# Low parts of weights on one engine, head factors inside the gates' product, four PSUM banks for the second half's gates, and a written order at the first modulation

## The chip, the cores and the metric

The kernel runs on one core of a Trainium2 chip. The metric is device time in microseconds for one execution, from launch to the last byte of the output in memory; of several executions the median is taken. The engines are named as in the profile: PE (TensorE) multiplies matrices and PEld loads its weights, DVE (VectorE) and ACT (ScalarE) do arithmetic on tiles, POOL (GpSimd) is the third engine that can do it, SP (SyncE) issues most DMAs. Each engine works through its own list of instructions strictly in order.

## The reference: what is computed

A decoder of two layers on 1024 tokens of width 1024, in float32. Cut to what matters here:

```python
cond = jax.nn.silu(c)
for l in range(DEPTH):                                   # l = 0: mixer A, l = 1: mixer B
    ada = cond @ ada_w[l] + ada_b[l]                     # six vectors of 1024
    sh1, sc1, g1, sh2, sc2, g2 = jnp.split(ada, 6, axis=-1)
    h = modulate(rmsnorm(x, norm_g[l, 0]), sh1, sc1)     # h * (1 + sc1) + sh1
    y = mlstm_mixer(h, ...) if l < N_A else mla_mixer(h, ..., k_nope, k_rope, v)
    x = x + g1 * rmsnorm(y, norm_g[l, 1])
    h = modulate(rmsnorm(x, norm_g[l, 2]), sh2, sc2)
    x = x + g2 * rmsnorm(jnp.square(jax.nn.relu(h @ w1)) @ w2, norm_g[l, 3])

# end of mlstm_mixer: q, k, v, ig, fg, og are columns of h @ w_in
hh = rmsnorm(hh.transpose(0, 2, 1, 3), head_g).reshape(B_, S, A_V_W)
return (hh * jax.nn.sigmoid(og)) @ w_out
```

Mixer A is a chunked mLSTM with 8 heads, mixer B a causal attention with 8 heads in which 128 queries at a time meet all earlier keys. `head_g` is one factor for each of the 1024 columns of `hh`.

## The kernel before

**Products in three passes.** Every operand of a large product is held as two numbers: a high part, which is the value cast to the type that PE multiplies, and a low part, which is the value minus the high part. One product is then three matmuls (`mm3`, lines 236 to 238): low times high, high times low, high times high. For a weight chunk of 128 by 1024 numbers (`raw`, 512 KB, brought by SP at L216) `wsplit` makes the two parts: ACT casts the high part `wh` (L193), and the low part `wl` is a subtraction (L195). Which engine subtracts is set by `low[0]`: DVE, POOL, or, while it is `None`, DVE and POOL by turns. It is set to DVE for the first weights, in the first MLP of the first half, and in the norms and projections of layer 1, to POOL in the attention of layer 1, and is `None` elsewhere. For activations `split_mod` does the same with a shift added: ACT writes the high part (L478), DVE the low part (L479).

**Halves and streams.** The 1024 tokens are worked on as two halves of 512 (`hfs[0]`, `hfs[1]`). Projections of a half run as "steps" of 128 output columns: 24 matmuls of 128x512 into one PSUM bank. Layer 0's mixer of the first half comes first, then that of the second half beside the first half's output projection; from the first MLP on, `two_streams` weaves a dense stream (an MLP of one half) with a second stream (the norms, projections and attention of the other half), and a third one of small background work is spread between (the adaLN products of later layers: chunks of `raw` multiplied by the conditioning vector on DVE, L363 and L365, summed by PE at L345 and DVE at L347).

**What sets the order.** The program is written as generators that are advanced by turns, and a planner puts each engine's instructions in order by a timeline that it keeps; `tc.high_priority` and `tc.issue_after(x)` (this instruction stands after x in the order) steer it. So a change of the engine of one operation moves others too. On the chip nothing is moved any more.

**PSUM.** There are three kinds of tiles, two of each: `ps` and `pc` of one bank, `pm` of two banks. `wout` (L890) with `wide` takes `ps` and the first bank of `pm` by turns, so that four steps are open at once.

**The four places of the change.**

- `wsplit` as above, with `follow[0]`: while it is set, the latest subtraction on DVE is what background work is paced by.
- `og0` (L671): the eight steps of the output gate of layer 0. Each step's product goes to a `ps` bank; ACT reads it (L676, exp), then does L677 (ln) and L678 (exp) in SBUF, which gives the sigmoid; DVE multiplies the tile by the head factor, a column of `cols` (L679). `split_o` (L786) later multiplies the mixer's output by the gate in blocks of two heads (L792, 128x1024), ACT casts the high part (L793), and DVE or POOL by turns subtracts (L794).
- `latent_weights` (L1153): six chunks are scaled by a row factor on POOL.
- `modulate0` (L1651): the first modulation. For each k, DVE multiplies x by the norm and the scale (L1655), and `split_mod` follows. The shift is the column `adac(0, SH1)`, which a DVE addition at L341 delivers (`ada`).

## Time and profile before

Three runs: median 2408.23 us (2406.89 to 2409.44). One execution was profiled.

| | before |
|---|---|
| median of 3 runs | 2408.23 us |
| the profiled execution's own time | 2411.54 us |
| its span (first to last instruction) | 2409.7 us |
| PE busy | 2367.1 us (98%) |
| DVE busy | 1481.7 us (61%) |
| ACT busy | 1051.8 us (44%) |
| POOL busy | 414.1 us (17%) |
| DMA, mean over the span | 155 GB/s |

The profiled execution took 1.84 us more than its span and 3.3 us more than the median; sums made from the trace are compared with 2411.54, and then carried over to the median. "Busy" of PE counts from the start of a matmul to its modelled end, and matmuls overlap, so 98% says that PE seldom stands, not that it runs at its peak. Line numbers are those of the kernel before; in the changed kernel the same lines stand two lines earlier up to the gates (L479 is L477 there), one earlier in the attention (L1128 is L1127), and L1655 is L1657.

### The profile page before, as it was taken

Reading aid. Unit: us, or ns where it says so; the run is one execution under the profiler, and the core shown is the slowest. Engines: PE = TensorE matmul, PEld = TensorE weight load, DVE = VectorE, ACT = ScalarE, POOL = GpSimd, SP = SyncE. Lnnn points to the kernel's source line nnn. Section 1 sums busy time; section 2 is a strip of 40 time slices with the busy share of each in tenths; the row PEclk is TensorE's granted clock in tenths of the full one; section 3 lists DMA queues with packets and bytes.
Section 4 is the critical chain, followed back from the end, with each engine's and each line's share of the span. In section 5 each row is a group of like instructions: output and inputs, shape, how many; then the busy total and the mean of one; then the engine's idle time right before and its main releaser. Section 6 shows DMA issues by size and latency. Waiting matters only on the chain.

```text
span 2409.7 us, 30573 instructions
## 1 busy us (share of the span) xinstructions
PE 2367.1 (98%) x11621; PEld 1947.3 (81%) x11621; DVE 1481.7 (61%) x2271; ACT 1051.8 (44%) x1712; POOL 414.1 (17%) x259
## 2 busy tenths in 40 slices
PE   7999999999999999999999999999999999999998
PEld 5888888788888887888888878888888888888887
DVE  6667766868665667866754967654555385253335
ACT  4355334555333454434443554434444443443333
POOL 2121111200000000234321100332221102121121
PEclk9999999999999999999999999999999999999999
DMA  8452654444654745455543444763424454354431
GB/s 305 144 149 81 188 179 132 144 144 149 184 175 140 249 131 189 153 164 179 181 131 114 144 163 161 238 241 133 158 97 137 116 162 123 109 188 133 144 104 62
DMA packets 377107, 374.49 MB, mean 155 GB/s; under 512 B 24355, under 2 KB 282464, under 8 KB 376960
## 3 DMA queue, kind: packets, MB, share of 16 engines
q1 hardware_dynamic: 376672, 372.44, 48.5%
q8 instruction: 92, 1.51, 0.3%
q14 instruction: 55, 0.45, 0.1%
q0 software_dynamic: 288, 0.10, 0.0%
HBM read 313.24 MB, written 59.24 MB: 155 GB/s over the span
## 4 chain that ended last, share of the span: by engine, by line
PE 89%; DVE 5%; DMA 3%; ACT 2%; issue 1%; SPq 0%; POOL 0%; DVEq 0%; ACTq 0%
PE ps L236 16%; PE ps L237 16%; PE ps L238 16%; PE pm L236 10%; PE pm L237 10%; PE pm L238 10%; DMA raw<-in_mlp_w_dram 1%; PE pc L1449 1%; PE pc L236 1%; PE pm L819 1%; PE pc L237 1%; PE pc L238 1%; PE pm L1335 1%; PE pm L1329 1%; PE pm L1331 1%
## 5 line engine op out<-in xcount | busy, mean ns | idle before, releaser
L193 ACT CAST wh<-raw 128x1024 fp32r<-128x1024 f32 (+2 forms) x366 | 375.8, 1031 | 724.0 <-PE ps L236 341.0
L195 POOL TENSOR_TENSOR wl<-raw,wh 128x1024 fp32r<-128x1024 f32 (+2 forms) x158 | 375.6, 2381 | 1558.6 <-ACT wh L193 1407.1
L236 PE MATMUL ps<-k,wl 128*128 128x512 f32 x1528 | 612.6, 401 | 6.1 <-ACT k L676 4.4
L237 PE MATMUL ps<-k,wh 128*128 128x512 f32 x1528 | 602.5, 394 | 0.0
L238 PE MATMUL ps<-k,wh 128*128 128x512 f32 x1528 | 602.4, 394 | 0.0
L195 DVE TENSOR_TENSOR wl<-raw,wh 128x1024 fp32r<-128x1024 f32 (+1 forms) x208 | 270.6, 1304 | 275.3 <-ACT wh L193 267.9
L236 PEld LDWEIGHTS ps<-k,wl 128*128 128x128 f32 x1528 | 288.0, 188 | 74.1 <-issue 7.2
L238 PEld LDWEIGHTS ps<-k,wh 128*128 128x128 f32 x1528 | 288.0, 188 | 67.6 <-issue 0.5
L237 PEld LDWEIGHTS ps<-k,wh 128*128 128x128 f32 x1528 | 288.3, 189 | 63.7 <-issue 1.7
L203 DVE TENSOR_TENSOR k<-k,pm 128x512 f32<-128x512 f32 (+1 forms) x254 | 210.5, 858 | 129.4 <-PE pm L238 128.8
L476 DVE TENSOR_TENSOR hd<-tmp,hd 128x512 fp32r<-128x512 f32 x128 | 120.7, 943 | 208.4 <-ACT hd L475 208.0
L236 PE MATMUL pm<-hd,wl 128*128 128x512 f32 x512 | 202.0, 394 | 0.5 <-ACT hd L475 0.5
L237 PE MATMUL pm<-hd,wh 128*128 128x512 f32 x512 | 199.4, 390 | 0.7 <-DVE hd L476 0.7
L238 PE MATMUL pm<-hd,wh 128*128 128x512 f32 x512 | 199.8, 391 | 0.0
L236 PE MATMUL pm<-wh,hd 128*128 128x512 f32 x488 | 193.0, 395 | 4.4 <-ACT raw L1341 4.2
L237 PE MATMUL pm<-wl,hd 128*128 128x512 f32 x488 | 190.9, 391 | 0.0
L238 PE MATMUL pm<-wh,hd 128*128 128x512 f32 x488 | 190.4, 390 | 0.0
L365 DVE SCALAR_TENSOR_TENSOR tma<-raw,cond,tma 128x512 f32<-128x512 f32 x168 | 129.1, 769 | 19.9 <-DMA raw<-in_kv_ada_w_dram 10.1
L1341 ACT ACTIVATE raw<-pm,sm 128x128 f32<-128x128 f32 (+3 forms) x64 | 47.5, 742 | 156.1 <-DVE sm L1340 126.8
L237 PEld LDWEIGHTS pm<-hd,wh 128*128 128x128 f32 x512 | 96.2, 188 | 21.7 <-DVE hd L476 1.0
L236 PEld LDWEIGHTS pm<-hd,wl 128*128 128x128 f32 x512 | 96.1, 188 | 21.2 <-ACT hd L475 0.9
L238 PEld LDWEIGHTS pm<-hd,wh 128*128 128x128 f32 x512 | 96.1, 188 | 21.1
(351 smaller groups left out, 3580.0 us busy)
## 6 DMA issues: line engine op xcount, KB each, us to landing
raw<-in_mlp_w_dram SPq DMA_DIRECT2D x256, 512.0 KB, 4.2
raw<-in_ada_w_dram SPq DMA_DIRECT2D x80, 512.0 KB, 4.3
raw<-in_a_w_in_dram SPq DMA_DIRECT2D x48, 512.0 KB, 4.6
xs<-k SPq DMA_DIRECT2D x40, 256.0 KB, 4.6
raw<-in_kv_ada_w_dram SPq DMA_DIRECT2D x16, 512.0 KB, 3.9
raw<-in_a_w_out_dram SPq DMA_DIRECT2D x16, 512.0 KB, 4.6
kd<-k SPq DMA_DIRECT2D x32, 256.0 KB, 3.7
vd<-k SPq DMA_DIRECT2D x32, 256.0 KB, 4.4
```

The lines of the kernel that those rows point to most:

```text
L193: nc.scalar.copy(hi[:, :n], r[:, :n])
L195: i = e.tensor_sub(lo[:, :n], r[:, :n], hi[:, :n].bitcast(F32))
L203: return f(*a, **k)
L236: nc.tensor.matmul(o, ll, rh, start=start, stop=False)
L237: nc.tensor.matmul(o, lh, rl, start=False, stop=False)
L238: pe_last[0] = nc.tensor.matmul(o, lh, rh, start=False, stop=stop)
L365: nc.vector.scalar_tensor_tensor(acc, r[:, kk], cond[:, k : k + 1], acc, ALU.mult, ALU.add)
L476: nc.vector.tensor_sub(lo, u, hi.bitcast(F32))
L819: nc.tensor.matmul(nv[:, r, i], hf.PT[p_][:, r, cs], v[:, 2 * p_ + r], start=g == 0, stop=True,)
L1329: nc.tensor.matmul(o[:, :w], ql, kh, start=True, stop=False)
L1331: nc.tensor.matmul(o[:, :w], qT, kk[1][:, ks], start=False, stop=False)
L1341: nc.scalar.activation(pr[:, :n], f, AF.Exp, bias=m, scale=SCALE, accum_out=l)
```

## The change

- Every `wl` is subtracted by DVE (`low` and `wcnt` are gone), and so are the second and fourth block of L794. The scaling of the six latent weights moves from POOL to DVE. POOL then has no arithmetic left but the setting of constants: its list has 96 rows where it had 264, DVE's has 2433 where it had 2273.
- The multiplication by the head factors (L679, 16 instructions of 128x512) goes. `split_o` does it in the same instruction as the gate: two `scalar_tensor_tensor` of 128x512 take the place of one product of 128x1024.
- `one_pm` names the first bank of a `pm` tile. In the second half, the odd steps of `og0` go there, the even ones to `ps`; in the first half all go to `ps` as before.
- `modulate0` writes down DVE's order: within a block of four k, the second product is put behind the addition that delivers the shift, the third behind the first low part, the fourth behind the second low part.

The diff, whole:

```diff
--- before.py
+++ after.py
@@ -153,6 +153,9 @@
     def pm():
         return pp.tile([P, 2, 512], F32, tag="pm", bufs=2, name=f"pm_{next(uid)}")
 
+    def one_pm():
+        return pm()[:, 0]
+
     def const(shape, dt, name):
         return sb.tile(shape, dt, tag=name, bufs=1, name=name)
 
@@ -183,17 +186,12 @@
 
         return tc.issue_after(pace[0]) if pace[0] else nullcontext()
 
-    wcnt = count()
-
-    low = [None]
-
     def wsplit(r, n):
         hi = sb.tile([P, 1024], F32R, tag="ws", bufs=WS, name=f"wh_{next(uid)}")
         lo = sb.tile([P, 1024], F32R, tag="ws", bufs=WS, name=f"wl_{next(uid)}")
         nc.scalar.copy(hi[:, :n], r[:, :n])
-        e = low[0] or (nc.gpsimd if next(wcnt) % 2 else nc.vector)
-        i = e.tensor_sub(lo[:, :n], r[:, :n], hi[:, :n].bitcast(F32))
-        if follow[0] and e is nc.vector:
+        i = nc.vector.tensor_sub(lo[:, :n], r[:, :n], hi[:, :n].bitcast(F32))
+        if follow[0]:
             pace[0] = i.ins
         return hi, lo
 
@@ -338,7 +336,7 @@
                 ada_last[0] = nc.tensor.matmul(
                     pt[:, j : j + 1], acc[:, ts(j, P)], ones[:, 0:1], start=True, stop=True
                 )
-            nc.vector.tensor_add(dst, pt[:, :4], bias)
+            ada_sum[0] = nc.vector.tensor_add(dst, pt[:, :4], bias)
             yield
             return
         for j in range(4):
@@ -348,7 +346,7 @@
         nc.vector.tensor_add(dst, s, bias)
         yield
 
-    ada_last = [None]
+    ada_last, ada_sum = [None], [None]
 
     def ada_chunk(w, c0, bias, dst, buf=raw):
 
@@ -671,12 +669,11 @@
     def og0(hf, alloc):
         hf.gs = FH(F32, alloc)
         for k in range(NH):
-            pt = proj_fm(w_in, 2064 + k * P, hf.h)
+            pt = proj_fm(w_in, 2064 + k * P, hf.h, one_pm if hf.i and k % 2 else ps)
             g = hf.gs[k]
             nc.scalar.activation(g, pt, AF.Exp, scale=-1.0)
             nc.scalar.activation(g, g, AF.Ln, bias=1.0)
             nc.scalar.activation(g, g, AF.Exp, scale=-1.0)
-            nc.vector.tensor_scalar(g, g, col(HG + k, 1), None, ALU.mult)
             yield
 
     c4 = lambda t: t[0:8].rearrange("p (c t) -> p c t", t=P)
@@ -788,10 +785,12 @@
         hf.o = Split()
         for b in range(4):
             o, g = hf.PT[b], hf.gs.t[b]
-            e = nc.gpsimd if b % 2 else nc.vector
-            nc.vector.tensor_mul(o, o, g)
+            for i in range(2):
+                nc.vector.scalar_tensor_tensor(
+                    o[:, i], o[:, i], col(HG + 2 * b + i, 1), g[:, i], ALU.mult, ALU.mult
+                )
             nc.scalar.copy(hf.o.hi.t[b], o)
-            e.tensor_sub(hf.o.lo.t[b], o, hf.o.hi.t[b].bitcast(F32))
+            nc.vector.tensor_sub(hf.o.lo.t[b], o, hf.o.hi.t[b].bitcast(F32))
             yield
 
     def chunks0(hf):
@@ -887,7 +886,7 @@
     def wout(w, o, store, wide=False):
 
         for m in range(KD):
-            pt = proj_fm(w, m * P, o, (lambda: pm()[:, 0]) if wide and m % 2 else ps)
+            pt = proj_fm(w, m * P, o, one_pm if wide and m % 2 else ps)
             store(m, pt)
             yield
 
@@ -1150,7 +1149,7 @@
                     nc.vector.scalar_tensor_tensor(
                         acc, r[:, k], sh[:, k : k + 1], acc, ALU.mult, ALU.add
                     )
-            nc.gpsimd.tensor_mul(r, r, A.unsqueeze(2).to_broadcast([P, KD, P]))
+            nc.vector.tensor_mul(r, r, A.unsqueeze(2).to_broadcast([P, KD, P]))
             for i, t in enumerate(wsplit(r_, D)):
                 nc.sync.dma_start(lw[b, i], t.bitcast(F32))
             yield "wait"
@@ -1650,10 +1649,14 @@
 
     def modulate0(h, xT, j):
         A, sh = A0, adac(0, SH1)
+
+        behind = [None, ada_sum[0].ins]
         for k in range(4 * j, 4 * j + 4):
             u = tmc()
-            nc.vector.scalar_tensor_tensor(u, xT[k], A[:, k : k + 1], rs0, ALU.mult, ALU.mult)
+            with tc.issue_after(behind[k % 4]) if behind[k % 4] else nullcontext():
+                nc.vector.scalar_tensor_tensor(u, xT[k], A[:, k : k + 1], rs0, ALU.mult, ALU.mult)
             split_mod(h.hi[k], h.lo[k], u, sh[:, k : k + 1])
+            behind.append(nc.cur_bb.bb.instructions[-1])
             yield
 
     def w_raw(b):
@@ -1672,13 +1675,11 @@
 
     w0 = [w_raw(b) for b in range(3)]
     hfs[0].h = Split()
-    low[0] = nc.vector
     w0[0] = w_parts(w0[0])
     drain(modulate0(hfs[0].h, xT0, 0))
     traced = nc.cur_bb.bb.instructions
     with tc.issue_after(next(i for i in reversed(traced) if i.engine == dve)):
         w0[1:] = [w_parts(r) for r in w0[1:]]
-    low[0] = None
     drain(ada_first(1, hd))
 
     def with_bg(g, bg, n):
@@ -1885,14 +1886,12 @@
             yield 1
 
     f0 = mlp(0, hfs[0], z0, [4] * 8)
-    low[0] = nc.vector
     for n in range(20):
         if next(f0) != "within":
             next(p1, None)
     drain(p1)
     two_streams(f0, behind(bg_latent(), 4))
     rope_perm()
-    low[0] = None
 
 
     z1 = FH(claim=True)
@@ -1903,23 +1902,18 @@
         lat = latent(hf, lambda: next(att))
         next(lat)
 
-        low[0] = nc.vector
         yield from to_x(hf, z)
         yield "fill"
         yield from lat
         yield next(att)
-        low[0] = nc.gpsimd
         yield from att
-        low[0] = None
         y = FH(claim=True)
         yield (1, 1)[hf.i]
         yield "align"
         for _ in wout(b_w_out[0], hf.o, lambda m, pt: evac(y[m], pt)):
             yield 0
-        low[0] = nc.vector
         yield 1
         yield from post(hf, y, B2, x_cols, A3, adac(1, SH2))
-        low[0] = None
 
     two_streams(mlp(0, hfs[1], z1, [2] * 14 + [4]), mixer1(hfs[0], z0, attention_first), bg_rest())
 
```

**The first modulation, DVE.** `tmc` is the product of x, norm and scale (L1655), `ada<-pc_269` the shift's addition, `k_49`, `k_51` the low parts of h (L479). Before:

```order
L1655 SCALAR_TENSOR_TENSOR tmc_294<-k_19_165,mods,Cst 128x512
L1655 SCALAR_TENSOR_TENSOR tmc_298<-k_19_165,mods,Cst 128x512
L1655 SCALAR_TENSOR_TENSOR tmc_302<-k_20_166,mods,Cst 128x512
L1655 SCALAR_TENSOR_TENSOR tmc_306<-k_20_166,mods,Cst 128x512
L195 TENSOR_TENSOR wl_291<-raw_276,wh_290 128x1024
L341 TENSOR_TENSOR ada<-pc_269,cols 128x4
L363 TENSOR_SCALAR tmc_318<-hd_319,cond 128x512
L365 SCALAR_TENSOR_TENSOR tmc_318<-hd_319,cond,tmc_318 128x512
L479 SCALAR_TENSOR_TENSOR k_49_283<-tmc_294,ada,k_48_282 128x512
L479 SCALAR_TENSOR_TENSOR k_49_283<-tmc_298,ada,k_48_282 128x512
```

With the change:

```order
L1657 SCALAR_TENSOR_TENSOR tmc_294<-k_19_165,mods,Cst 128x512
L193 TENSOR_TENSOR wl_291<-raw_276,wh_290 128x1024
L339 TENSOR_TENSOR ada<-pc_269,cols 128x4
L1657 SCALAR_TENSOR_TENSOR tmc_298<-k_19_165,mods,Cst 128x512
L477 SCALAR_TENSOR_TENSOR k_49_283<-tmc_294,ada,k_48_282 128x512
L1657 SCALAR_TENSOR_TENSOR tmc_302<-k_20_166,mods,Cst 128x512
L477 SCALAR_TENSOR_TENSOR k_49_283<-tmc_298,ada,k_48_282 128x512
L1657 SCALAR_TENSOR_TENSOR tmc_306<-k_20_166,mods,Cst 128x512
L361 TENSOR_SCALAR tmc_318<-hd_319,cond 128x512
L477 SCALAR_TENSOR_TENSOR k_51_285<-tmc_302,ada,k_50_284 128x512
```

The shift's addition stood behind four products and a `wl`; now it stands behind one product and the `wl`, and low parts come between the products.

**The second half's gates, ACT, from the fourth step's gate on** (casts of weights, the later steps of a gate and one square are left out). `k<-ps` or `k<-pm` are the first reads of a step's bank; `tmc<-hd` are squares for the norm of the first half's residual, whose sums DVE makes. Before:

```order
L676 ACTIVATE k_646_3879<-ps_4058 128x512
L458 ACTIVATE tmc_4191<-hd_3283 128x512
L458 ACTIVATE tmc_4193<-hd_3283 128x512
L458 ACTIVATE tmc_4199<-hd_3284 128x512
L458 ACTIVATE tmc_4202<-hd_3285 128x512
L458 ACTIVATE tmc_4205<-hd_3285 128x512
L458 ACTIVATE tmc_4208<-hd_3286 128x512
L793 CAST k_665_3967<-hd_2572 128x1024
L458 ACTIVATE tmc_4211<-hd_3286 128x512
L676 ACTIVATE k_647_3880<-ps_4112 128x512
L676 ACTIVATE k_647_3880<-ps_4159 128x512
L676 ACTIVATE k_648_3881<-ps_4220 128x512
```

With the change:

```order
L674 ACTIVATE k_646_3875<-pm_4052 128x512
L456 ACTIVATE tmc_4184<-hd_3279 128x512
L456 ACTIVATE tmc_4186<-hd_3279 128x512
L456 ACTIVATE tmc_4189<-hd_3280 128x512
L792 CAST k_665_3961<-hd_2568 128x1024
L456 ACTIVATE tmc_4192<-hd_3280 128x512
L674 ACTIVATE k_647_3876<-ps_4106 128x512
L674 ACTIVATE k_647_3876<-pm_4152 128x512
L456 ACTIVATE tmc_4195<-hd_3281 128x512
L456 ACTIVATE tmc_4198<-hd_3281 128x512
L456 ACTIVATE tmc_4201<-hd_3282 128x512
L674 ACTIVATE k_648_3877<-ps_4213 128x512
```

The reads of the fifth and sixth step (`k_647`) still stand behind squares, behind four instead of eight, and behind the cast of a block of the mixer's output; the banks change too: `ps_4106`, `pm_4152`, `ps_4213` where it was `ps_4112`, `ps_4159`, `ps_4220`.

**A block of attention in the first half, DVE, ahead of the sum that the scores wait for.** `tma<-raw` is background work, `hd<-tmp` the low part of the MLP's hidden block, the last row the MLP's sum (L203) that frees a `pm` tile. Before:

```order
L365 SCALAR_TENSOR_TENSOR tma_9586<-raw_9595,cond,tma_9586 128x512
L476 TENSOR_TENSOR k_1661_9635<-ps_9636,k_1661_9635 128x512
L365 SCALAR_TENSOR_TENSOR tma_9586<-raw_9595,cond,tma_9586 128x512
L1127 TENSOR_TENSOR tmc_9664<-pc_9661,hd_7687 128x512
L476 TENSOR_TENSOR k_1663_9648<-pc_9649,k_1663_9648 128x512
L1128 TENSOR_TENSOR tmc_9516<-tmc_9516,tmc_9664 128x512
L1312 CAST k_1667_9667<-tmp_9668 64x512
L1314 TENSOR_TENSOR k_1667_9667<-tmc_9516,tmp_9668 64x512
L476 TENSOR_TENSOR hd_9680<-tmp_9706,hd_9680 128x512
L203 TENSOR_TENSOR k_1208_7294<-k_1208_7294,pm_9717 128x1024
```

With the change:

```order
L363 SCALAR_TENSOR_TENSOR tma_9578<-raw_9583,cond,tma_9578 128x512
L474 TENSOR_TENSOR k_1661_9627<-ps_9628,k_1661_9627 128x512
L363 SCALAR_TENSOR_TENSOR tma_9578<-raw_9583,cond,tma_9578 128x512
L193 TENSOR_TENSOR wl_9669<-raw_9666,wh_9668 128x1024
L363 SCALAR_TENSOR_TENSOR tma_9578<-raw_9587,cond,tma_9578 128x512
L1126 TENSOR_TENSOR tmc_9656<-pc_9653,hd_7679 128x512
L474 TENSOR_TENSOR k_1663_9640<-pc_9641,k_1663_9640 128x512
L363 SCALAR_TENSOR_TENSOR tma_9578<-raw_9587,cond,tma_9578 128x512
L193 TENSOR_TENSOR wl_9706<-raw_9703,wh_9705 128x1024
L1127 TENSOR_TENSOR tmc_9508<-tmc_9508,tmc_9656 128x512
L1311 CAST k_1667_9659<-tmp_9660 64x512
L201 TENSOR_TENSOR k_1208_7286<-k_1208_7286,pm_9709 128x1024
```

Two subtractions, which POOL made beside these rows, now stand among them, and two of the background rows stand later.

## The prediction, before the result was known

> **What bounds the kernel now.** First the page's table of engines, then the list of PE's waits, then the busy time by windows with the granted clock, last the timeline at each place that the waits name.
>
> ```profile
> PE 2367.1 (98%) x11621; PEld 1947.3 (81%) x11621; DVE 1481.7 (61%) x2271; ACT 1051.8 (44%) x1712; POOL 414.1 (17%) x259
> PE ps L236 <- ACT k L676: 4.4, 1, 4.4
> ...
> PE pm L236 <- ACT raw L1341: 4.2, 5, 1.7
> PE pm L1329 <- DVE k L203: 2.8, 3, 1.2
> ```
>
> PE is busy for 2367.1 of a span of 2409.7 us, so it bounds the kernel, and a change of DVE's or POOL's work can only move the 42.6 us in which PE stands, plus what slow clock follows. The change doesn't touch PE's work, so its worth is read place by place. The clock:
>
> ```profile
> 27.00:34.00 7.00, 5.92 (x15) 3.19 (x16) 6.96 (x12) 3.50 (x5) 0.00 (x0) 0.56 1.05 388
> 254.98:258.40 3.42, 1.72 (x26) 1.48 (x23) 2.39 (x3) 2.58 (x6) 0.00 (x0) 1.00 0.82 249
> 258.40:261.81 3.41, 3.41 (x10) 2.65 (x9) 1.45 (x3) 1.04 (x1) 0.33 (x1) 0.50 0.88 281
> 439.31:446.14 6.83, 4.76 (x11) 3.79 (x12) 6.83 (x10) 4.49 (x8) 2.54 (x1) 0.50 0.27 82
> ```
>
> The columns are busy times of PE, PEld, DVE, ACT and POOL, then the granted clock. After stretches of 3.4 us in which PE stood about half the time or more, the next ones are granted half clock. PE's busy time at half clock is worth half: 3.41 / 2 = 1.7 us lost at 258, 4.76 / 2 = 2.4 us at 439. So a wait costs more than its own length when it fills half of such a stretch.
>
> **Part 1: the low parts.**
>
> ```profile
> L195 POOL TENSOR_TENSOR wl<-raw,wh 128x1024 fp32r<-128x1024 f32 (+2 forms) x158 | 375.6, 2381 | 1558.6 <-ACT wh L193 1407.1
> L195 DVE TENSOR_TENSOR wl<-raw,wh 128x1024 fp32r<-128x1024 f32 (+1 forms) x208 | 270.6, 1304 | 275.3 <-ACT wh L193 267.9
> 1123.35 1.92 DVE L1128 TENSOR_TENSOR tmc<-tmc,tmc 128x512 f32<-128x512 f32 x1
> 1124.83 2.72 POOL L195 TENSOR_TENSOR wl<-raw,wh 128x1024 fp32r<-128x1024 f32 x1
> 1125.95 2.01 DVE L1312 CAST k<-tmp 64x512 fp32r<-64x512 f32 x1 [0.69 <-ACT tmp L1310]
> 1127.98 0.43 DVE L1313 CAST k<-tmp 64x512 fp32r<-64x512 f32 x1
> ```
>
> A subtraction takes 2381 ns on POOL and 1304 ns on DVE, 1.21 us in the undisturbed row at 256.76 below. 158 of them add 158 x 1.21 = 191 us to DVE, which has 2409.7 - 1481.7 = 928 us idle: as a total it fits (about 1673 us, 69%). It gets something back: while POOL subtracts, DVE's instructions stretch. The cast at 1125.95 began inside POOL's subtraction and took 2.01 us; its like at 1127.98, when POOL was done, took 0.43. So some of the 191 us comes back, which I count only where PE waits.
>
> Where does it matter? (a) At 116 us:
>
> ```profile
> 115.00 1.05 ACT L193 CAST wh<-raw 128x1024 fp32r<-128x1024 f32 x1 [0.73 <-DMA raw<-in_a_w_in_dram]
> ...
> 116.13 2.84 POOL L195 TENSOR_TENSOR wl<-raw,wh 128x1024 fp32r<-128x1024 f32 x1 [34.95 <-ACT wh L193]
> 119.02 0.39 PE L237 MATMUL ps<-wl,k 128*128 128x256 f32 x1 [1.26 <-POOL wl L195]
> ```
>
> The cast ends at 116.05 and POOL's subtraction at 118.97. On DVE, 1.21 us from the cast's end, it ends at about 117.3, 1.7 us earlier, which is more than PE's gap of 1.26. I take 1.2; bounds 0 and 1.7.
>
> (b) At 236 to 262, in `split_o` of the first half:
>
> ```profile
> 236.75 5.94 POOL L794 TENSOR_TENSOR k<-hd,k 128x1024 fp32r<-128x1024 f32 x2 [4.86 <-ACT k L793]
> 237.91 2.39 DVE L716 TENSOR_TENSOR mcol<-tmc,tmc 8x1 f32<-8x1 f32 x1
> 240.34 2.62 DVE L712 TENSOR_TENSOR_SCAN tmc<-ones,mcol,tmc 8x128 f32<-8x128 f32 x1
> 243.18 0.47 DVE L712 TENSOR_TENSOR_SCAN tmc<-ones,mcol,tmc 8x128 f32<-8x128 f32 x1
> 251.78 0.37 SPq L216 DMA_DIRECT2D raw<-in_a_w_in_dram  x1
> 255.68 1.04 ACT L193 CAST wh<-raw 128x1024 fp32r<-128x1024 f32 x1 [2.52 <-DMA raw<-in_a_w_in_dram]
> 256.76 1.23 DVE L195 TENSOR_TENSOR wl<-raw,wh 128x1024 fp32r<-128x1024 f32 x1 [1.03 <-ACT wh L193]
> 258.04 0.52 PE L236 MATMUL ps<-k,wl 128*128 128x512 f32 x1 [1.70 <-DVE wl L195]
> ```
>
> Read backwards: PE stood 1.70 us for a `wl`, that for the cast, that for a DMA issued at 251.78, that for a `raw` tile which DVE's background work had to free. DVE was late because POOL's two L794 held it: a scan of 0.47 us took 2.62, and a row of 8x1 elements 2.39. Against these 2.15 + 2.2 us stand two more L794 at about 1.2 and the splitting of L792, some 3 us on DVE; and in the new order the background rows stand ahead of the chain's last rows. I expect the issue 2 us earlier, enough for the whole wait of 1.70, and with it for the half clock after it, 1.7: together 3.4. Bounds: 0, and 4.1 with the 0.7 that PE stands shortly before.
>
> The Trainium skill ("TensorE: Matmul & The Clock Gate", section "Why this matters for your kernels") says that no idle gap over about 3 us should be left, since one idle window halves the rate. By it a wait of 1.70 us would not have halved the clock, this place would be worth 1.7 us, and the median 2396.1; the row 258.40:261.81 with 0.50 says otherwise, so I go by the trace.
>
> (c) Attention of layer 1, first half, three blocks alike:
>
> ```profile
> 1120.73 0.68 DVE L1127 TENSOR_TENSOR tmc<-pc,hd 128x512 f32<-128x512 f32 x1
> 1121.18 1.05 ACT L193 CAST wh<-raw 128x1024 fp32r<-128x1024 f32 x1 [3.62 <-DMA raw<-in_mlp_w_dram]
> 1130.45 2.34 DVE L203 TENSOR_TENSOR k<-k,pm 128x1024 f32<-128x1024 f32 x2
> 1131.72 0.39 PE L1329 MATMUL pm<-k,k 128*128 128x256 f32 x1 [1.22 <-DVE k L203]
> ```
>
> PE waits for the sum at 1130.45, the last row of a DVE chain. The two stretched rows above, L1128 (about 0.7 unblocked, by its likes of the same shape) and L1312, give back 1.2 + 1.6 = 2.8 us. Against it stand two subtractions, 2.4, now in the chain. The first waits for a cast that ends at 1122.23, while L1127 behind it began at 1120.73: 1122.23 + 1.2 - 1120.73 = 2.7 late, of which DVE's idle time before 1122.74 (1.33) takes a half. So +2.4 + 0.3 - 2.8, near nothing: I take a gain of 0.1 a block, 0.3 in all. Bounds: the 2.8 of the waits list won, or 1.0 lost a block.
>
> (d) Attention of the second half: the 4.2 us for L1341 (softmax) hang on DVE rows that are stretched in the same way, and subtractions come among them too. As (c) comes out near nothing I take 0.7 won; bounds 1.5 lost (0.3 late in each of five blocks) and the whole 4.2. (e) Elsewhere PE has no wait, and how much room DVE's rows have there isn't seen: a `wl` that waits for its cast could make them late by the 2.7 of (c). I set 0.5 aside as lost; bound 3.
>
> **Part 2: heads' factors, four banks (400 to 480 us).**
>
> ```profile
> 432.68 4.12 POOL L195 TENSOR_TENSOR wl<-raw,wh 128x1024 fp32r<-128x1024 f32 x1 [9.67 <-ACT wh L193]
> 434.47 2.61 DVE L679 TENSOR_SCALAR k<-k,cols 128x512 f32<-128x512 f32 x1
> 437.71 0.63 ACT L458 ACTIVATE tmc<-hd 128x512 f32<-128x512 f32 x1 [4.06 <-DVE tmc L462]
> 440.66 1.06 ACT L676 ACTIVATE k<-ps 128x512 f32<-128x512 f32 x2
> 441.38 0.76 PE L236 MATMUL ps<-k,wl 128*128 128x512 f32 x1 [4.41 <-ACT k L676]
> ```
>
> PE stood 4.41 us because both `ps` banks were full: their reader, ACT's L676 at 440.66, stood behind squares (L458), and ACT stood 4.06 us for DVE, which was in L679, 2.61 us long under POOL's subtraction (0.47 without one, by L363 at 27.19 below). The change takes away three links: L679 is gone, POOL doesn't subtract, and the seventh step goes to the bank of the third, not the fifth. What ACT's late read holds up is then the first output step, two steps later: 48 matmuls or 11 us (0.23 us each, by 480.00 us for 2094 in Part 4). So the wait goes, 4.41, and the half clock behind it, 2.4: 6.8. New work on DVE there (two halves of 0.74 for one L792 of 1.21, two subtractions and one L794) is about as long as the L679s and the stretching that go. Next late would be the second half's `split_o`: its last block hangs on the last gate by six instructions of 0.6 to 1.2 us, and PE reads it after four output steps on the other blocks, 72 matmuls or 16 us. Bounds 4.0 (a gap of 1.2 us stays and is followed by half clock) and 7.5.
>
> **Part 3: first modulation.**
>
> ```profile
> 23.33 2.74 DVE L1655 SCALAR_TENSOR_TENSOR tmc<-k,mods,Cst 128x512 f32<-128x512 f32 x4
> 27.12 0.15 DVE L341 TENSOR_TENSOR ada<-pc,cols 128x4 f32<-128x4 f32 x1
> 27.19 0.47 DVE L363 TENSOR_SCALAR tmc<-hd,cond 128x512 f32<-128x512 f32 x1
> 27.30 1.95 ACT L478 ACTIVATE k<-tmc,ada 128x512 fp32r<-128x512 f32 x3 [2.48 <-DVE ada L341]
> 28.08 0.79 PE L236 MATMUL pm<-k,wl 128*128 128x512 f32 x1 [4.36 <-ACT k L478]
> ```
>
> The shift at 27.12 stood behind four products, 2.74 us; now behind one: 2.74 x 3/4 = 2.0 earlier, and PE starts at about 26.1. The clock there is 0.56, so the early matmuls run at half clock: at worst 2.0 brings 1.0; if the earlier start also ends the slow stretch earlier, up to 2.6. I take 1.9. Two low parts wait for nothing more than before.
>
> **Part 4: latent weights.** Six products go to DVE in a stretch in which PE has no gap (480 to 960 us: PE busy 480.00 of 480.00): 0.
>
> ```profile
> 480.00:960.00 480.00, 480.00 (x2094) 389.83 (x2093) 320.21 (x438) 217.42 (x298) 13.10 (x11) 1.00 0.55 170
> ```
>
> DVE is busy for 320 of those 480 us, so six more at about 1.2 us don't show.
>
> **Sum**: 1.2 + 3.4 + 0.3 + 0.7 - 0.5 + 6.8 + 1.9 + 0 = 13.8 us. Against the profiled execution's own 2411.5 this is 2397.7; that execution is 3.3 us over the median, so the median comes to 2408.2 - 13.8 = **2394.4 us**.
>
> **Rivals.** *R1, the waits are only handed on.* ACT still reads the fifth and sixth gate behind squares that wait for DVE, and the `raw` tile of (b) is held by another reader. Then Part 2 pays 4.0 and (b) nothing, the early start 1.0, (a) 1.2: 6.2 us, 2402.0. For it: the squares still stand ahead in ACT's order. Against: the bank is wanted two steps later.
> *R2, DVE's order becomes the limit, the slower side.* A subtraction that is first in DVE's list blocks everything behind it until its weight is in. In the eight blocks of both attentions that are tight (three for L203, five for L1341) the 2.7 us worked out in (c) would pass to PE instead of being absorbed: 8 x 2.7 = 21.6 lost against 13.8 + 0.5 - 1.0 = 13.3 won elsewhere, 2416.5. It decides from 13.3 / 8 = 1.7 us a block. For it: the new order of the block, and a cast that waited 3.62 us for its DMA. Against: the rows that get shorter by 2.8 a block.
> *R3, the change does not reach the path.* If the wait at 441 comes back through `split_o`, (b) is lost as in R1 and the start is held by its DMAs (share 1.05 at 27 to 34), (a)'s 1.2 and 1.0 of the start remain: 2406.0.
>
> **Numbers.** A difference under 0.2%, 4.8 us, can't be told from none here. Forecast 0.68, its own range 2388 to 2400; R1 0.14; R3 0.10; R2 0.08. R1's 2402 is faster by 6.2, mostly beyond the bound: faster 0.68 + 0.12, same 0.02 + 0.10 and some of R2, slower 0.07. The range reaches from 2387 (all upper bounds together, 22.9 us, would give 2385) to 2404, which takes in R1.
>
> **What would show it.** Right: no wait for L676 around 437 and a granted clock of 1.00 from 439 to 446; no half clock at 258; PE's first product of h about 2 us earlier; DVE at 65 to 70%; the cast L1312 at about 0.43. Wrong: PE waiting for DVE (`k` L203, `wl` L195) in the attentions for longer than 2.8 us; a new wait at 441 for another releaser.

## The result, and the profile after

| | before | changed |
|---|---|---|
| median (all runs of the two beside each other) | 2408.64 us (6 runs, 2406.89 to 2411.41) | 2394.71 us (6 runs, 2392.80 to 2396.81) |
| the profiled execution's own time, span | 2411.54, 2409.7 us | 2392.80, 2391.0 us |
| DVE, POOL busy | 1481.7, 414.1 us | 1549.9, 18.2 us |

The ratio is 0.9941, 95% interval 0.9928 to 0.9954: 13.9 us faster by the medians. A later set of five runs of the same kernel gave 2395.72 us and 0.9941 again. The profiled executions lie 18.7 us apart: that of before was 2.9 us over its median, that of the changed kernel is the fastest of its six. So sums over the two traces give some 5 us more than the medians.

The page's table of engines, and the list of PE's waits of the changed kernel (left out are waits for the first DMAs and constants, and some of 1.0 us or less):

```profile
PE 2365.1 (99%) x11621; PEld 1945.3 (81%) x11621; DVE 1549.9 (65%) x2431; ACT 1055.2 (44%) x1712; POOL 18.2 (1%) x91
...
PE pm L234 <- ACT k L476: 2.4, 1, 2.4
PE pm L234 <- ACT raw L1340: 1.6, 3, 1.1
...
PE ps L234 <- DVE wl L193: 0.8, 1, 0.8
...
PE pm L1330 <- DMA k<-td: 0.4, 1, 0.4
...
PE pm L1328 <- DVE k L201: 0.2, 1, 0.2
```

PE stands 2391.0 - 2365.1 = 25.9 us where it stood 42.6. The waits for L676 (4.4) and for POOL's low part (1.3) have no successor in the list, that for the first modulation fell from 4.4 to 2.4, L1341 (now L1340) from 4.2 to 1.6, the MLP's sum from 2.8 to 0.2. A new one of 0.8 for a `wl` stands at 269 us. DVE took on 158 subtractions, 191 us by the prediction's price, and is busy only 68 us longer.

Three groups of DVE's instructions, by shape, of the changed kernel (count, total us, mean ns, idle time before):

```profile
L193 DVE TENSOR_TENSOR wl<-raw,wh 128x1024 fp32r<-128x1024 f32 x350 | 426.7, 1222 | 433.2 <-ACT wh L192 427.0 <-PE ps L236 2.9 <-DMA k<-in_x_dram 1.5
L474 DVE TENSOR_TENSOR hd<-tmp,hd 128x512 fp32r<-128x512 f32 x128 | 88.3, 690 | 57.0 <-ACT hd L473 56.7
L1127 DVE TENSOR_TENSOR tmc<-tmc,tmc 128x512 f32<-128x512 f32 x10 | 6.8, 685 | 0.1
```

and of the kernel before:

```profile
L195 DVE TENSOR_TENSOR wl<-raw,wh 128x1024 fp32r<-128x1024 f32 x204 | 267.5, 1314 | 273.2 <-ACT wh L193 267.6 <-PE ps L238 4.7 <-DMA lw<-wl 0.6
L476 DVE TENSOR_TENSOR hd<-tmp,hd 128x512 fp32r<-128x512 f32 x128 | 120.7, 943 | 208.4 <-ACT hd L475 208.0
L1128 DVE TENSOR_TENSOR tmc<-tmc,tmc 128x512 f32<-128x512 f32 x10 | 13.9, 1394 | 0.1
```

The same work takes 690 ns where it took 943, 685 where it took 1394. That is where most of the missing 120 us went: DVE had been held while POOL subtracted. These three groups account for 58 us of it, all groups with the same line and shape in both lists for about 110 (the shorter mean, times the smaller count).

The first modulation in the changed kernel's timeline (start, length, engine, line; rows between are left out):

```profile
22.89 0.75 DVE L1657 SCALAR_TENSOR_TENSOR tmc<-k,mods,Cst 128x512 f32<-128x512 f32 x1
23.56 1.22 DVE L193 TENSOR_TENSOR wl<-raw,wh 128x1024 fp32r<-128x1024 f32 x1
24.69 0.15 DVE L339 TENSOR_TENSOR ada<-pc,cols 128x4 f32<-128x4 f32 x1
...
25.66 0.74 PE L234 MATMUL pm<-k,wl 128*128 128x512 f32 x1 [2.38 <-ACT k L476]
```

The shift is there at 24.69, 27.12 before, and PE starts at 25.66, 28.08 before: 2.4 us. Of these, 0.4 are not the change's: the first product itself starts at 22.89, and before at 23.33. Busy time and clock by windows (PE, PEld, DVE, ACT, POOL, clock, DMA), first at the start, then at the gates and in the stretch of `split_o`:

```profile
25.00:32.00 7.00, 6.29 (x19) 3.47 (x20) 6.87 (x11) 3.65 (x5) 0.00 (x0) 0.76 1.05 388
400.00:480.00 80.00, 80.00 (x346) 64.24 (x345) 60.94 (x81) 50.05 (x75) 0.79 (x8) 1.00 0.54 172
252.90:256.30 3.40, 3.40 (x26) 2.53 (x23) 2.83 (x4) 2.32 (x10) 0.00 (x0) 1.00 0.92 251
256.30:259.70 3.40, 3.40 (x17) 2.74 (x16) 1.23 (x1) 0.90 (x1) 0.00 (x0) 1.00 0.64 222
```

At the start the clock is 0.76 in this profile; in e8, the same kernel once more, it is 0.53 in the same window, so that is no gain of the change. Between 400 and 480 us, and around 256, PE never stands and has full clock throughout.

### The profile page after: what moved, and what is told of

It reads as the page before. It is cut to its first block, busy times and chain, and to the rows that moved or that the text cites. A ratio compares the mean times of both kernels' runs of the same rounds, so it can differ in the third digit from the quotient of the medians.

```text
span 2391.0 us, 30521 instructions
## 1 busy us (share of the span) xinstructions
PE 2365.1 (99%) x11621; PEld 1945.3 (81%) x11621; DVE 1549.9 (65%) x2431; ACT 1055.2 (44%) x1712; POOL 18.2 (1%) x91
## 4 chain that ended last, share of the span: by engine, by line
PE 92%; DVE 3%; DMA 3%; ACT 1%; issue 1%; SPq 0%; DVEq 0%; ACTq 0%
PE ps L234 17%; PE ps L236 16%; PE ps L235 16%; PE pm L234 10%; PE pm L235 10%; PE pm L236 10%; PE pc L1448 1%; PE pc L234 1%; PE pc L235 1%; PE pc L236 1%; PE pm L1334 1%; PE pm L818 1%; DMA raw<-in_mlp_w_dram 1%; DMA raw<-in_a_w_in_dram 1%; PE pm L1328 1%
## 5 line engine op out<-in xcount | busy, mean ns | idle before, releaser
L193 DVE TENSOR_TENSOR wl<-raw,wh 128x1024 fp32r<-128x1024 f32 (+2 forms) x366 | 438.7, 1202 | 437.4 <-ACT wh L192 428.5
L234 PE MATMUL ps<-k,wl 128*128 128x512 f32 x1496 | 598.3, 400 | 0.9 <-DVE wl L193 0.8
L236 PE MATMUL ps<-k,wh 128*128 128x512 f32 x1496 | 588.8, 394 | 0.0
L235 PE MATMUL ps<-k,wh 128*128 128x512 f32 x1496 | 587.1, 392 | 0.0
L236 PEld LDWEIGHTS ps<-k,wh 128*128 128x128 f32 x1496 | 280.9, 188 | 66.5 <-issue 0.2
L234 PEld LDWEIGHTS ps<-k,wl 128*128 128x128 f32 x1496 | 281.0, 188 | 65.9 <-issue 2.7
L235 PEld LDWEIGHTS ps<-k,wh 128*128 128x128 f32 x1496 | 281.4, 188 | 62.2 <-issue 1.4
L363 DVE SCALAR_TENSOR_TENSOR tma<-raw,cond,tma 128x512 f32<-128x512 f32 x168 | 125.6, 748 | 20.1 <-DMA raw<-in_kv_ada_w_dram 13.5
L474 DVE TENSOR_TENSOR hd<-tmp,hd 128x512 fp32r<-128x512 f32 x128 | 88.3, 690 | 57.0 <-ACT hd L473 56.7
L1340 ACT ACTIVATE raw<-pm,sm 128x128 f32<-128x128 f32 (+3 forms) x64 | 47.5, 742 | 151.3 <-DVE sm L1339 129.2
L960 ACT ACTIVATE tmp<-ps 128x512 f32<-128x512 f32 x128 | 75.8, 592 | 83.5 <-PE ps L236 83.4
```

The lines of the kernel that those rows point to most:

```text
L193: i = nc.vector.tensor_sub(lo[:, :n], r[:, :n], hi[:, :n].bitcast(F32))
L234: nc.tensor.matmul(o, ll, rh, start=start, stop=False)
L235: nc.tensor.matmul(o, lh, rl, start=False, stop=False)
L236: pe_last[0] = nc.tensor.matmul(o, lh, rh, start=False, stop=stop)
L363: nc.vector.scalar_tensor_tensor(acc, r[:, kk], cond[:, k : k + 1], acc, ALU.mult, ALU.add)
L474: nc.vector.tensor_sub(lo, u, hi.bitcast(F32))
```

## The experiments

Ten kernels, each beside runs of the kernel before. "Against changed" is the difference of the two ratios times 2409 us; the intervals are about 0.0013 wide to either side, 3 us, so that differences of 2 us are weak by themselves.

| run | median us | ratio to before, 95% interval | against changed |
|---|---|---|---|
| changed, again (e8) | 2395.72 | 0.9941 [0.9928, 0.9953] | 0 |
| e1: POOL works for nothing in the attentions | 2420.68 | 1.0048 [1.0035, 1.0060] | +25.8 |
| e2: no written order | 2397.85 | 0.9951 [0.9938, 0.9963] | +2.4 |
| e3: two banks | 2399.80 | 0.9962 [0.9949, 0.9974] | +5.1 |
| e4: low parts as before | 2403.17 | 0.9976 [0.9967, 0.9986] | +8.4 |
| e7: head factors apart | 2397.37 | 0.9949 [0.9936, 0.9961] | +1.9 |
| e9: POOL in the first attention | 2400.24 | 0.9959 [0.9947, 0.9972] | +4.3 |
| e10: POOL in the second attention | 2396.31 | 0.9945 [0.9931, 0.9958] | +1.0 |
| e5: before, low parts on DVE alone | 2400.26 | 0.9960 [0.9947, 0.9973] | +4.6 |
| e6: before, four banks alone | 2411.03 | 1.0007 [0.9998, 1.0017] | +15.9 |

### e1: is it POOL's hold on DVE, or its slow subtraction?

The changed kernel with the old settings of `low[0]`, which only this reads; the results in `RM` are used by nobody.

```diff
         i = nc.vector.tensor_sub(lo[:, :n], r[:, :n], hi[:, :n].bitcast(F32))
+        if low[0] is nc.gpsimd:              # in the attentions, as before
+            for c0 in range(0, n, 512):
+                w_ = min(512, n - c0)
+                h_ = hi[:, c0 : c0 + w_].bitcast(F32)
+                nc.gpsimd.tensor_sub(RM[:, :w_], h_, h_)
```

> The changed kernel with one thing more: in the attentions of layer 1, wherever the kernel before had POOL subtract a low part, POOL now subtracts a high part from itself into a tile that nobody reads (two pieces of 512 columns). The order on PE, DVE, ACT and SP is that of the changed kernel. Theory: in the attentions POOL cost time by stretching DVE's instructions, not by delivering its own low parts late. It expects stretched DVE rows in 960 to 1250 and 1500 to 1850 us (mean of the low part of the MLP's hidden block from 0.69 back to 0.9 us or more), PE's waits for the softmax's exponent back from 1.6 to about 4 us, and a kernel slower than the changed one by 4 to 8 us. Rival: what helped was that DVE delivers a low part in 1.2 us where POOL took 2.4. It expects the same stretched rows but a time within 1.5 us of the changed kernel.

Measured: 2420.68 us, 26 us slower than the changed kernel and 11 slower than the kernel before. The theory's direction holds (POOL's results are used by nobody, so lateness of a low part is out, and in e1's list of waits nothing waits for L200), its size does not. The timeline of one block of the first attention:

```profile
1123.95 1.23 DVE L195 TENSOR_TENSOR wl<-raw,wh 128x1024 fp32r<-128x1024 f32 x1 [1.97 <-ACT wh L194]
1124.00 2.07 POOL L200 TENSOR_TENSOR RM<-wh 128x512 fp32r<-128x512 f32 x1 [6.88 <-ACT wh L194]
...
1126.18 3.91 POOL L200 TENSOR_TENSOR RM<-wh 128x512 fp32r<-128x512 f32 x3
...
1129.11 2.06 DVE L195 TENSOR_TENSOR wl<-raw,wh 128x1024 fp32r<-128x1024 f32 x1
...
1136.62 0.39 PE L1335 MATMUL pm<-k,k 128*128 128x256 f32 x1 [3.98 <-DVE k L208]
```

Each holds the other: POOL's first piece takes 2.07 us while DVE's subtraction runs, DVE's second takes 2.06. PE's wait for the sum is 3.98 us, where it was 1.22 before and at most 0.2 in the changed kernel's list. Four such waits sum to 12.2 us, and a lower clock follows (0.69 from 1136 to 1139.5 us). The two profiled executions lie 28.7 us apart; about 23 of these arise between 960 and 1250 us, 3 in the second attention and 2.4 ahead of both, read from how far the starts of the same matmuls have drifted apart. Two expectations failed: the mean of the low part of the hidden block went to 0.77, not to 0.9 or more, and the waits for the softmax's exponent sum to 1.3 us, not to 4.

### e9 and e10: how much of it in which attention?

```diff
         yield next(att)
+        if hf.i == 0:                        # e10: hf.i == 1
+            low[0] = nc.gpsimd               # wsplit subtracts on low[0]
         yield from att
+        low[0] = nc.vector
```

> The changed kernel with the low parts of the first half's attention alone (40 of them, all that POOL subtracted there) back on POOL; nothing moves outside 960 to 1250 us. Theory, from the two profiles: low parts on DVE brought 2.3 us here; so 1.5 to 3 us slower than the changed kernel, with the three waits for the MLP's sum back at about 1 us each. Rival, the prediction's step: 0.3 us, no difference that can be measured.

> The changed kernel with the low parts of the second half's attention alone (40) back on POOL; nothing moves outside 1500 to 1850 us. Theory, from the two profiles: they brought 5.0 us here, of which up to 1.5 may be a DMA wait that varies; so 3 to 5.5 us slower than the changed kernel, the waits for the softmax's exponent back from 1.6 to about 4 us. Rival, the prediction's step: 0.7 us.

Measured: e9 is 4.3 us slower than the changed kernel, e10 1.0. In e9 the three waits are back (`pm L1330 <- DVE k L203` sums to 3.4 us), and its trace and the changed kernel's drift apart by about 3 us in the stretch; the rest of its profile's surplus came later, in a stretch that was not touched, with a wait of 1.8 us for a reloaded tile. So the first attention is worth 3 to 4 us, more than the theory's 2.3 and ten times the prediction's 0.3. The second is worth 1 to 1.5: the softmax waits rose to 2.7 us, not 4, and the 5.0 us by which the two profiles differ there were for the most part not POOL's. A block of e9, to be read against the same rows of the changed kernel:

```profile
1114.45 2.42 POOL L195 TENSOR_TENSOR wl<-raw,wh 128x1024 fp32r<-128x1024 f32 x1 [7.56 <-ACT wh L194]
1115.50 1.92 DVE L1129 TENSOR_TENSOR tmc<-tmc,tmc 128x512 f32<-128x512 f32 x1
1116.97 2.71 POOL L195 TENSOR_TENSOR wl<-raw,wh 128x1024 fp32r<-128x1024 f32 x1
1118.10 2.00 DVE L1313 CAST k<-tmp 64x512 fp32r<-64x512 f32 x1 [0.69 <-ACT tmp L1311]
1123.85 0.39 PE L1330 MATMUL pm<-k,k 128*128 128x256 f32 x1 [1.55 <-DVE k L203]
```

The changed kernel:

```profile
1101.92 0.48 DVE L361 TENSOR_SCALAR tma<-raw,cond 128x512 f32<-128x512 f32 x1
1102.32 1.22 DVE L193 TENSOR_TENSOR wl<-raw,wh 128x1024 fp32r<-128x1024 f32 x1
1103.57 0.38 SPq L214 DMA_DIRECT2D raw<-in_mlp_w_dram  x1
...
1107.90 1.05 ACT L192 CAST wh<-raw 128x1024 fp32r<-128x1024 f32 x1 [1.60 <-DMA raw<-in_mlp_w_dram]
1108.98 1.23 DVE L193 TENSOR_TENSOR wl<-raw,wh 128x1024 fp32r<-128x1024 f32 x1 [1.30 <-ACT wh L192]
1113.78 0.69 DVE L1127 TENSOR_TENSOR tmc<-tmc,tmc 128x512 f32<-128x512 f32 x1
1118.05 2.47 DVE L201 TENSOR_TENSOR k<-k,pm 128x1024 f32<-128x1024 f32 x2
1119.32 0.39 PE L1328 MATMUL pm<-k,k 128*128 128x256 f32 x1
```

and the kernel before, at the same place:

```profile
1112.77 2.41 POOL L195 TENSOR_TENSOR wl<-raw,wh 128x1024 fp32r<-128x1024 f32 x1 [7.03 <-ACT wh L193]
1113.23 2.23 DVE L363 TENSOR_SCALAR tma<-raw,cond 128x512 f32<-128x512 f32 x1
1115.49 0.75 DVE L365 SCALAR_TENSOR_TENSOR tma<-raw,cond,tma 128x512 f32<-128x512 f32 x1
1116.27 1.01 SPq L216 DMA_DIRECT2D raw<-in_mlp_w_dram  x2
```

Ahead of this block the traces are 11.3 us apart. So the weight's DMA, issued at 1116.27 before (1105.0 on the changed kernel's clock), goes out 1.4 us earlier, right after the subtraction at 1102.32 has ended, and the cast starts at 1107.90 instead of 1109.9. The lists of SP's waits say what held each issue. In the changed kernel it is the subtraction (`SPq L214 <- DVE wl L193`, 6.2 us). Before, it is a row of background work (`SPq L216 <- DVE tma L365`, 7.4 us), and this row stood behind the L363 above, which took 2.23 us under POOL's subtraction and 0.48 in the changed kernel. No run tests this link by itself.

### e4 and e5: the low parts, taken away and alone

e4 is the changed kernel with the old `wsplit`, its `low[0]` settings, L794 and L1153 on POOL as before; e5 the kernel before with this alone:

```diff
-        e = low[0] or (nc.gpsimd if next(wcnt) % 2 else nc.vector)
-        i = e.tensor_sub(lo[:, :n], r[:, :n], hi[:, :n].bitcast(F32))
-        if follow[0] and e is nc.vector:
+        i = nc.vector.tensor_sub(lo[:, :n], r[:, :n], hi[:, :n].bitcast(F32))
+        if follow[0]:
...
-            e = nc.gpsimd if b % 2 else nc.vector
+            e = nc.vector
...
-            nc.gpsimd.tensor_mul(r, r, A.unsqueeze(2).to_broadcast([P, KD, P]))
+            nc.vector.tensor_mul(r, r, A.unsqueeze(2).to_broadcast([P, KD, P]))
```

> The changed kernel with the low parts, the second and fourth block of the mixer's low parts and the latent weights back on POOL as before; written order, head factors and four banks stay. By the differences between the two profiles the low parts on DVE are worth 2 us at 236 to 262, 2.3 in the first attention and 5 in the second: 8 to 11 us slower than the changed kernel. Rival: the four banks and the written order are worth more, and this part under 5 us.

> The kernel before with nothing but the low parts, all blocks of the mixer's low parts and the latent weights on DVE; head factors as their own instruction, two banks and the planner's own order at the first modulation stay. Theory: POOL's hold on DVE also made most of the wait at 437 us (with two banks and all else of the change only 1.4 us of it came back), so this part alone brings the 8.5 us that its removal cost and some 5 of the gates' 6.8: about 2395 to 2398 us, and a wait under 2 us at the gates. Rival: the parts add up; then it brings 8.5, about 2400.5, and the wait at the gates stays over 3 us.

Measured: without them 8.4 us slower than the changed kernel; alone 8.1 us faster than before by the medians (2408.35 to 2400.26; 9.6 by the ratio). So they are the largest part whichever way they are taken, and the rival of e5, that the parts add up, holds on the sum: its 2400.26 is the 2400.5 of the rival, not the 2395 to 2398 of the theory. At the gates e5 has a wait of 2.8 us (4.4 before), which fits neither: the theory wanted under 2, the rival over 3.

### e3, e6, e7: what the gates' place needs

```diff
 # e3, the changed kernel but
-            pt = proj_fm(w_in, 2064 + k * P, hf.h, one_pm if hf.i and k % 2 else ps)
+            pt = proj_fm(w_in, 2064 + k * P, hf.h, ps)
 # e6, the kernel before but
-            pt = proj_fm(w_in, 2064 + k * P, hf.h)
+            pt = proj_fm(w_in, 2064 + k * P, hf.h, (lambda: pm()[:, 0]) if hf.i and k % 2 else ps)
 # e7, the changed kernel but
+            nc.vector.tensor_scalar(g, g, col(HG + k, 1), None, ALU.mult)      # in og0
+            nc.vector.tensor_mul(o, o, g)                                      # in split_o, for the two halves
```

> The changed kernel with the second half's gates all in ps, two banks, as before; rows move only between 430 and 480 us. Theory A: the banks end the wait (the late read by ACT is still there); PE stands again 3 to 4.5 us at about 433 us and runs at half clock behind it, 5 to 7 us slower than the changed kernel. Theory B: the wait was made by DVE, stretched under POOL and with the head factors in its list; with both gone ACT reads in time and two banks are enough: under 2 us slower, clock 1.00 around 435 us.

> The kernel before with nothing but the odd gate steps of the second half in the first bank of pm. ACT's read of the fifth step is as late as it was. Theory: the bank is then wanted two steps (11 us) later, so the wait of 4.4 and the half clock behind it go although DVE is as stretched as before: 5 to 7 us faster than before, about 2402 to 2404. Rival: the wait comes back at the output steps or the second block of split_o, and under 3 us are won.

> The changed kernel with the head factors multiplied in as before: eight instructions of 128x512 more for each half on DVE (0.48 us each), one product of 128x1024 instead of two of 128x512 in each block. Theory: with POOL quiet they take 0.48 and not 2.6 us and hide behind four banks: within 1.5 us of the changed kernel. Rival: they stand ahead of the sums that ACT's squares wait for, and a wait of over 1.5 us shows at 420 to 445 us: 2 to 4 us slower.

e3 is 5.1 us slower, but at the gates PE stands only 1.4 us and keeps full clock. So the place is as theory B had it, and the time as theory A had it, for another reason: the rest arose elsewhere, at 696 us, where a wait for background work came up with half clock behind it. What links it to the banks is open; of the other runs only e7 waits there. Windows of e3, at the gates and there:

```profile
432.40:435.80 3.40, 2.04 (x11) 1.48 (x10) 3.40 (x6) 2.79 (x5) 0.00 (x0) 1.00 0.87 300
435.80:439.20 3.40, 3.40 (x17) 2.75 (x16) 3.40 (x6) 2.35 (x5) 0.00 (x0) 1.00 0.94 288
694.00:697.50 3.50, 1.59 (x9) 1.30 (x9) 3.50 (x5) 2.90 (x5) 0.00 (x0) 0.97 0.48 147
697.50:701.00 3.50, 3.50 (x10) 2.68 (x10) 3.36 (x6) 0.00 (x0) 0.00 (x0) 0.54 1.08 316
```

e6 is the run that went against its theory: no difference from before. The wait for L676 is gone, as expected, and by 468 us its trace is 8.5 us ahead of that of before (1.7 of them since before 400 us, where this edit moves nothing); by 484 all of it is lost again, as its rival had it. The list of PE's waits and the timeline of e6:

```profile
PE ps L236 <- POOL wl L195: 6.5, 1, 6.5
466.64 5.39 DVE L479 SCALAR_TENSOR_TENSOR k<-hd,ada,k 128x512 fp32r<-128x512 f32 x8
468.51 10.26 POOL L195 TENSOR_TENSOR wl<-raw,wh 128x1024 fp32r<-128x1024 f32 x2 [7.48 <-ACT wh L193]
476.45 3.40 DVE L195 TENSOR_TENSOR wl<-raw,wh 128x1024 fp32r<-128x1024 f32 x1
```

PE reached the output steps earlier, and there two of POOL's subtractions, begun under a run of DVE's low parts, took 10.26 us together, and a subtraction of DVE's own under them 3.40. PE waited 6.5 us. But for four banks to pay, DVE need not make all the low parts. In e4 POOL subtracts as before, in this stretch too (22.17 us busy), and beside the order in the first 60 us its program differs from that of e6 by the folded head factors alone. Its list has no wait of PE between 400 and 490 us, and the window shows full clock:

```profile
400.00:490.00 90.00, 90.00 (x393) 72.53 (x392) 70.55 (x82) 55.70 (x85) 22.17 (x16) 1.00 0.54 168
```

e4 is also 7.5 us faster than e6 by the ratios.

e7 is 1.9 us slower by the ratios, too near the limit to call; its trace shows a wait of 0.3 us for a `wl` in this stretch and one of 1.0 us at about 695 us. So with the low parts on DVE the folded factors were not shown to bring anything; with some of them on POOL they decide whether four banks pay. Any two of the three measures leave at most 1.4 us of the wait (e3, e4, e7), four banks or low parts alone leave or move more (e6, e5). The folded factors alone were not run.

### e2 and e8: the written order, and the changed kernel once more

```diff
-            with tc.issue_after(behind[k % 4]) if behind[k % 4] else nullcontext():
+            with nullcontext():
```

> The changed kernel without the written order at the first modulation; only a few rows of DVE and PE in the first 60 us move. Theory: the early addition of the shift is worth 2.4 us in the profile; so PE's first product of h goes back from 25.7 to about 28 us and the kernel is 1.5 to 3 us slower than the changed one. Rival: with the low parts on DVE the planner puts the addition early anyway, or the early start is eaten by later waits: under 0.5 us.

> The changed kernel once more, for a second profile and five more times. The two kernels' profiles differ by 18.7 us and their medians by 13.9, so some terms must vary from run to run. Theory: what varies is waits for DMAs (start, reloaded tiles near 1590 us) and the windows of half clock behind them; the waits for DVE and ACT are the same within 0.5 us. Then this profile's span lies at 2391 to 2395, and the surplus over 2391.0 shows at such places. Rival: every place varies a little.

In e2 DVE's first product of the modulation starts at 22.87 us, as in the changed kernel (22.89), and PE's first product of `h` at 27.63 instead of 25.66. So the written order brings 2.0 us at this place. But little of it lasts. Rows of e2, then of e8, and e8's wait at 39 us:

```profile
27.63 0.79 PE L234 MATMUL pm<-k,wl 128*128 128x512 f32 x1 [4.36 <-ACT k L476]
25.78 0.80 PE L234 MATMUL pm<-k,wl 128*128 128x512 f32 x1 [2.38 <-ACT k L476]
PE pc L336 <- DVE tmc L363: 0.9, 1, 0.9
```

Seven of the eight profiles with the written order have this wait, 0.5 to 0.9 us long; the first profile of the changed kernel alone has not. When the mixer's first matmul starts (L772 before), the early start is nearly gone: at 74.6, 74.7, 74.4 and 74.2 us without the written order (before, e2, e5, e6), at 72.8 and 74.1 in the changed kernel's two profiles, and at 75.3, 73.7, 74.7, 73.0, 75.9 and 75.1 in e1, e3, e4, e7, e9 and e10. The means are 74.5 and 74.3. By the times e2 is 2.4 us slower by the ratios, 3.1 by the medians (2397.85 to 2394.71), which is within the intervals. So the traces speak for the rival, that the early start is eaten by later waits, and the worth of the written order is not shown.

e8's span is 2393.3 us, and the surplus of 2.3 lies at 40 us (the wait above, and half clock for longer), at 147 (a wait for ACT's `k`, 1.1 instead of 0.4) and at 1590 (the reloaded tile, 1.1 instead of 0.4). Two of these are waits for DVE and ACT that differ by more than 0.5 us, against the theory; it was right on the span and on the reloaded tile. Ten of the twelve profiles have that wait at 1590, 0.4 to 1.9 us long; the lists of e6 and e10 do not have it. So a single pair of traces can't size a place to better than 1 us, and the two that were compared first lay on opposite sides.

## Why the prediction was right, and where its steps were not

The time, 2394.71, is within 0.3 us of the forecast of 2394.4. That it is so near is luck: errors of the steps cancel. In the table, a lead is how much earlier the same matmuls start than in the profile of before. The figures say by how much it grows over a stretch, in the first and the second profile of the changed kernel.

| step | taken | measured |
|---|---|---|
| first modulation | 1.9 | first product of `h` 2.0 earlier; about 0.2 left at 75 us; times +2.4, within the noise (e2) |
| (a) 116 us | 1.2 | its gap of 1.26 is gone; the lead grows by 1.3 there and has lost that by 148 us |
| (b) `split_o` | 3.4 | gaps and half clock gone, a new wait of 0.8 at 269; lead 2.3 and 2.3 (230 to 290 us) |
| gates, Part 2 | 6.8 | no wait, full clock; lead 6.7 and 6.7 (380 to 520 us) |
| (c) first attention | 0.3 | lead 2.5 and 2.2; 3 to 4.3 (e9) |
| (d) second attention | 0.7 | 1.0 to 1.5 (e10) |
| (e), latent weights | -0.5 | nothing seen to lose there |

The measured column comes to 13 to 15. The start and (a) were taken at 3.1 and left next to nothing, (b) was taken 1 too high, and the attentions brought some 3 to 5 more than was taken.

**First modulation**: the 2.0 us were reasoned rightly (the start at "about 26.1" came at 25.66 because the whole chain began 0.4 earlier). What failed is that 1.9 of them were taken to last: PE met a wait for background work at about 39 us (e8). **(b)**: the chain read backwards held: the weight's DMA goes out at 247.70, which is 2.6 us earlier than before when the lead of 1.5 is taken off. By the rule of the Trainium skill that the prediction weighed ("TensorE: Matmul & The Clock Gate", section "Why this matters for your kernels") the wait of 1.70 us would have cost no clock, and the trace of before does not agree. But the half clock behind it was a near thing. The profile of before has a gap of 1.72 us at 1637.62 too, with full clock behind it (the first two windows), and so has e6 behind the same wait as in (b), 1.64 us there (the last two):

```profile
1633.97:1637.39 3.42, 1.93 (x12) 1.46 (x10) 1.24 (x2) 1.97 (x5) 1.99 (x1) 1.00 0.66 208
1637.39:1640.80 3.41, 3.01 (x12) 2.18 (x12) 3.06 (x7) 1.17 (x5) 0.00 (x0) 1.00 0.33 99
254.26:257.67 3.41, 1.77 (x24) 1.53 (x21) 2.44 (x3) 2.57 (x6) 0.00 (x0) 1.00 0.85 251
257.67:261.09 3.42, 3.42 (x16) 2.76 (x16) 1.30 (x3) 1.05 (x1) 0.60 (x1) 1.00 0.92 265
```

PE was busy for 1.93 and 1.77 us of these windows; in (b) before it was 1.72, and the next window had half clock. In e4 a wait of 1.63 us costs no clock either. So the 1.7 us of half clock in (b) were a cost of the profiled execution; whether the kernel before pays it as a rule is open.

**Part 2** had the right sum, but no one of the links that it named does it alone. The prediction let the wait go because L679 is gone, POOL doesn't subtract, and "the seventh step goes to the bank of the third, not the fifth". With the other two links in place, two banks leave a wait of 1.4 us (e3); low parts on DVE alone leave 2.8 (e5); four banks alone move the loss 35 us on (e6); four banks with the folded factors are enough, with POOL still subtracting (e4). e6 is what R1 said of handing on, though at another place, and the change is not e6.

**(c)** is the step that was mis-sized: "near nothing: I take a gain of 0.1 a block". It charged the two subtractions with 2.4 us and let the first wait for a cast at the time that it had before. But the cast's DMA went out 1.4 us earlier, and the cast came 2.0 us earlier, so the first subtraction found a part of DVE's idle time. The step had counted the rows that POOL stretched behind the cast, and not the one ahead of it (L363) that held back its DMA. The bound given, 2.8 us, was reached. (d) is too small as well; whether for the same reason stays open.

**R2**, the slower side, needed 1.7 us lost a block. e1 shows that DVE's order in the attention is indeed on the edge: the same order, with POOL busy beside it, costs 26 us. It is POOL's silence that makes it bearable. R3 fell with the first listing of waits. The signs named for "right" all came: no L676, clock 1.00 from 439 to 446 and at 258, DVE at 65%, the casts L1311 and L1312 at 0.42 us.

## What to carry to other kernels

An engine that looks idle and helps out can cost more than it does: price its work by what the neighbour's instructions take under it (here 690 ns became 943), and by the DMAs that start when its inputs come free. More buffers at one wait are worth what the next wait leaves of them; e6 won 6.8 us at the gates and had lost them 16 us later. An earlier start is worth what is left of it behind the next wait; of 2.0 us at the first modulation some tenths were. And before a place is sized to a microsecond, look at it in a second profile of the same kernel.

## What the runs showed of the hardware that was not expected

The hold between DVE and POOL goes both ways, and it adds up: two subtractions on POOL that take about 2.4 us each took 10.26 together beside DVE's low parts (e6). PE's clock was halved after gaps of 1.70 and 1.91 us, in windows of 3.4 to 3.5 us with PE busy for 1.72 and 1.59; gaps of 1.72 us (before, at 1637) with 1.93 us busy, of 1.64 (e6) with 1.77 and of 1.4 (e3) with 2.04 left it at 1.00. So in these places it was the busy part of the window, about half of it, that decided, and not the gap's length: 1.70 us halved the clock and 1.72 did not. It is not the whole rule: at 42 us e1, e9 and e10 show half clock behind windows of 3.4 us in which PE was busy for 3.1 to 3.2.
